# Low parts of the down weights on DVE, and weight blocks added by an accumulating load in the last three passes

## The chip, the cores and the metric

The kernel runs on one core of one Trainium2 chip. A core has TensorE (PE, matmuls; PEld is its weight load), VectorE (DVE), ScalarE (ACT), GpSimd (POOL) and SyncE (SP, which here only issues DMAs). SP's and POOL's DMAs go through two different queues, and each of those two works through its own instructions in order, as every engine does. The metric is device time of one execution in microseconds (us); lower is better.

## The reference, cut to what matters

The reference is one layer of a diffusion backbone: a token mixer, then a gated channel mixer (ConvGLU) whose result is normalised, scaled and added to the residual. The change lies in the last product, of the gated activations with the down weights. With 1024 tokens, a model width of 1024 and `D_FF` = 2816, and all arithmetic in fp32:

```python
g = silu(dwconv2d(h @ w_up[:, :D_FF])) * (h @ w_up[:, D_FF:])
y = g @ w_down                  # (1024, 2816) @ (2816, 1024)
out = x1 + gate * rmsnorm(y)
```

(The names are shortened here; the order of the operations is the reference's.)

## The kernel before

**The down projection.** It is the kernel's last stage. The product is tiled 2 by 2 over the two halves of the tokens and the two halves of the output columns, and 2 by 2 over the 2816 inner rows as well (22 blocks of 128, in two halves of `NJ` = 11). Instead of 8 products of halves it takes 7, by Strassen's scheme: `PASSES` lists for each of the 7 passes which parts of G (the gated activations) and which parts of the down weights are summed or subtracted. A pass has 11 steps, one for each block of 128 inner rows, so the stage has 77 steps, numbered n = 11 x pass + j. Two weight blocks are combined in passes 1 and 2 (a difference) and 4, 5 and 6 (a sum); two blocks of G in passes 0, 3, 4, 5 and 6.

**A step.** `prep(n)` makes the operands and `mm(n, t)` uses them. fp32 accuracy is reached by splitting each operand into a high part, rounded to the matmul's fp32r format, and a low part, the remainder, and by three matmuls for each product (`mm3`, lines 191 to 193: high x high, high x low, low x high). For each of 4 token tiles t that is 12 matmuls a step, 128 x 128 by 128 x 512. `prep(n)` issues in this order: one or two loads of a 128 x 512 weight block (256 KB) into the two halves of a buffer `raw` (line 1589, on SP's queue); where two were loaded, DVE's sum or difference into the first half (line 1591); ACT's copy of it to `wh`, the high part (line 1598); POOL's subtraction `wl` = raw - wh, the low part (line 1599, which appears in the trace as line 165, where the helper `sub_l` stands); then for G the sum on DVE (line 1603), ACT's copy (line 1606) and DVE's low part (line 165 again, with `pg` as its output).

**Buffers.** `raw` is one of the two buffers of tag `raw` (called `wr` in the trace) in every fourth step, and otherwise a page of a pool of 36 pages (`pg`), which also holds the blocks of G, their high and low parts, and the results of passes. `wh` and `wl` have four buffers each. The last six steps of pass 6 take pages for `wh` and `wl` too and are run tile by tile (all six steps for t = 0, then for t = 1, and so on), so that output tiles become ready one after the other.

**Order.** `prep` is called five steps ahead of the matmuls, the first four of them among the last steps of the up projection; a scheduler of the framework then fixes one order for each engine and the semaphores between them. Around the start of the stage DVE still computes the last 3 x 3 convolution (line 1471, nine steps in a row over the buffer `cv`), after which ACT's silu (line 1475) gives the last gated block. From pass 2 on POOL has 24 operations on results of passes (line 1448: four each of M4 - M5, C01 - C10, F + M4 and M1 + M4, and eight products with a gate). The work on results is held in a list `late`, of which a step pops one.

**Names in the rows.** `pg`, `wr` and `s`, `m`, `pad` are buffers, `ps` is a PSUM bank, `wh` and `wl` are the weights' parts, `gd` is the gated activations kept in DRAM.

Of the kernel before, what the change touches and what calls it, by code (L numbers as in the profile page):

```python
# [13 lines left out]
ALU = mybir.AluOpType  # L14
# [4 lines left out]
P = 128  # L19
# [81 lines left out]
class Kern:  # L101
# [1323 lines left out]
    def ffn(self):  # L1425
        nc, tc, A = self.nc, self.tc, self.A
        V = nc.vector
        wu = A["w_up"][0].rearrange("(k p) n -> p k n", p=P)
        with tc.tile_pool(name="ffn", bufs=1, reuse_waits="tile") as fp:
# [134 lines left out]
            def gpart(f, i):  # L1564

                if f not in here:
                    here[f] = [f >= NF - 5] * 2
                    if not here[f][0]:
                        g[f] = self.pg()
                c = slice(512 * i, 512 * i + 512)  # L1570
                if not here[f][i]:
                    nc.sync.dma_start(g[f][:, c], gd[f][:, c])
                    here[f][i] = True
                return g[f][:, c]

            def prep(n):

                ps, j = divmod(n, NJ)
                ga, wa = PASSES[ps]
                if ps == 4 and j == 0:  # L1580
                    self.gp2 = self.pg()
                    nc.sync.dma_start(self.gp2, self.gp[1])
                if n % 4:
                    raw = self.pg().rearrange("p (a n) -> p a n", a=2)
                else:
                    raw = self.wp.tile([P, 2, 512], F32, tag="raw", bufs=2, name=self.nm("wr"))
                for x, (k, c, _) in enumerate(wa):
                    f = j + NJ * k
                    nc.sync.dma_start(raw[:, x], A["w_down"][0, f * P:(f + 1) * P, 512 * c:512 * c + 512])
                if len(wa) > 1:  # L1590
                    V.tensor_tensor(raw[:, 0], raw[:, 0], raw[:, 1], op=ALU.add if wa[1][2] > 0 else ALU.subtract)
                if ps == 6 and j >= NJ - 6:
                    hl = self.page2()
                    wh, wl = hl[:, 0], hl[:, 1]
                else:
                    wh = self.wp.tile([P, 512], F32R, tag="wh", bufs=4, name=self.nm("wh"))
                    wl = self.wp.tile([P, 512], F32R, tag="wl", bufs=4, name=self.nm("wl"))
                nc.scalar.copy(wh, raw[:, 0])
                self.sub_l(nc.gpsimd, wl, raw[:, 0], wh)
                src = [gpart(j + NJ * k, i) for i, k, _ in ga]  # L1600
                if len(ga) > 1:
                    tmp = big("s") if ps == 0 else tmps[n % 4]
                    V.tensor_tensor(tmp, src[0], src[1], op=ALU.add if ga[1][2] > 0 else ALU.subtract)
                    src = [tmp]
                gs = self.page2()
                nc.scalar.copy(gs[:, 0], src[0])  # L1606
                self.sub_l(V, gs[:, 1], src[0], gs[:, 0])
                return gs, wh, wl
# [74 lines left out]
            for n, (f, p) in enumerate(seq):  # L1683
# [6 lines left out]
                x = st.setdefault(f, {})  # L1690
# [3 lines left out]
                ps = x[bank]  # L1694
                h, l = W.pop((f, p))
                for d in range(4):
                    c = slice(d * P, d * P + P)
# [24 lines left out]
                if n >= len(seq) - 4:  # L1722
                    i = len(ops)
                    ops[i] = prep(i)
            work(len(back))
            for i in range(5):
                if i not in ops:
                    ops[i] = prep(i)
# [45 lines left out]
            for ps in range(7):  # L1774
                bk = banks[BSET[ps]]
                for j in range(NJ):
                    n = ps * NJ + j
                    a = 5
                    if ps == 6 and j >= 5:
                        a += j - 5 + 1  # L1780
                    for i in range(n + 5, min(n + a, NS - 1) + 1):
                        if i not in ops:
                            ops[i] = prep(i)
                    if n < NS - 6:
                        for t in range(4):
                            mm(n, t)
                    if late and j > 0 and (ps < 6 or len(late) > 4 or j % 5 == 5 - 1):
                        late.pop(0)()
                    if ps in (5, 6) and j >= NJ - 5 and len(ahead) < 4 * (ps - 4):
                        load_x1(len(ahead))  # L1790
# [69 lines left out]
```

## Time and profile before

| | |
|---|---|
| time, median of 3 runs | 1411.86 us (1411.44 to 1413.65) |
| the profiled execution's own time | 1411.65 us |
| its span in the trace | 1409.9 us |
| mean granted clock of TensorE, whole span | 0.978 |
| the stage in question | about 1142 us to the end |

The page gives busy times over the whole span, as sums for each engine and for groups of instructions by line. The trace behind it gives the same by stretches of time, every instruction in order with the idle time before it and what ended that idle time, and for a DMA the time from issue to landing. A granted clock of 1.00 is TensorE's higher level of 2.4 GHz; a mean below it is a mix with the lower level of 1.2 GHz.

### The profile page before, as it was taken

How to read it: one execution, taken by the hardware profiler on the slowest of the kernel's cores; microseconds unless marked ns; L12 is line 12 of the kernel's file. 1: busy time of each engine (PE TensorE's matmuls, PEld its weight loads, DVE VectorE, ACT ScalarE, POOL GpSimd, SP SyncE). 2: the span in 40 equal slices, each digit the busy share in tenths (PEclk: the TensorE clock that was granted, in tenths of full speed). 3: DMA queues.
4: the chain of work that ended last, by engine and by line, in shares of the span. 5: the costliest groups of instructions: out<-in, count | busy, mean ns of one | idle time of the engine just before them, and what ended most of it. 6: DMA issues, size and time to landing. Idle time of an engine off the chain costs nothing.

```text
span 1409.9 us, 19321 instructions
## 1 busy us (share of the span) xinstructions
PE 1296.7 (92%) x6678; PEld 1028.1 (73%) x6678; DVE 1044.1 (74%) x1715; ACT 614.2 (44%) x1292; POOL 675.5 (48%) x593
## 2 busy tenths in 40 slices
PE   5999999989899999989988999999999989998685
PEld 2677876566566889877866777888888877886564
DVE  3675556836855847865688888888887899799977
ACT  5343456433543234345354344444444445454432
POOL 0440123232351354345365666666666647656773
PEclk9999999999999999999999999999999999999988
DMA  9522237676386778542403133222332285443454
GB/s 326 175 97 82 69 90 219 206 202 210 137 235 226 256 237 268 182 143 86 156 21 87 63 90 90 76 90 75 90 90 75 78 268 192 162 142 122 141 209 179
DMA packets 181427, 209.47 MB, mean 149 GB/s; under 512 B 31383, under 2 KB 119505, under 8 KB 181329
## 3 DMA queue, kind: packets, MB, share of 16 engines
q1 hardware_dynamic: 180465, 205.09, 45.2%
q0 software_dynamic: 864, 3.15, 0.7%
q8 instruction: 53, 0.87, 0.2%
q14 instruction: 45, 0.37, 0.1%
HBM read 161.01 MB, written 47.19 MB: 148 GB/s over the span
## 4 chain that ended last, share of the span: by engine, by line
PE 43%; DVE 17%; DMA 5%; issue 5%; POOL 5%; ACT 3%; SPq 0%; DVEq 0%; ACTq 0%; POOLq 0%
PE ps L191 11%; PE ps L192 11%; PE ps L193 11%; PE ps L1081 3%; POOL wl L165 2%; DVE cv L1471 2%; DVE pg L165 2%; PE ps L1025 1%; DVE T L982 1%; DVE s L1448 1%; POOL pg L165 1%; DVE pg L984 1%; PE ps L305 1%; DVE pg L1756 1%; POOL pg L1006 1%
## 5 line engine op out<-in xcount | busy, mean ns | idle before, releaser
L191 PE MATMUL ps<-pg,wh 128*128 128x512 f32 (+1 forms) x896 | 352.8, 394 | 13.2 <-ACT m L1703 10.0
L193 PE MATMUL ps<-pg,wl 128*128 128x512 f32 (+1 forms) x896 | 348.2, 389 | 0.6 <-POOL wl L165 0.6
L192 PE MATMUL ps<-pg,wh 128*128 128x512 f32 (+1 forms) x896 | 347.6, 388 | 0.0
L1471 DVE SCALAR_TENSOR_TENSOR cv<-pad,dw,cv 128x1024 f32<-128x1024 f32 x176 | 226.4, 1286 | 16.5 <-ACT cv L1469 13.1
L191 PEld LDWEIGHTS ps<-pg,wh 128*128 128x128 f32 x896 | 170.0, 190 | 62.9 <-issue 15.0
L165 POOL TENSOR_TENSOR wl<-wr,wh 128x512 fp32r<-128x512 f32 x86 | 126.2, 1472 | 179.8 <-ACT wh L183 123.7
L193 PEld LDWEIGHTS ps<-pg,wl 128*128 128x128 f32 x896 | 170.7, 190 | 37.1 <-issue 3.5
L192 PEld LDWEIGHTS ps<-pg,wh 128*128 128x128 f32 x896 | 170.7, 190 | 31.2 <-issue 0.4
L165 POOL TENSOR_TENSOR wl<-pg,wh 128x512 fp32r<-128x512 f32 x83 | 124.1, 1499 | 98.7 <-ACT wh L1641 54.1
L165 POOL TENSOR_TENSOR wl<-s,wh 128x512 fp32r<-128x512 f32 x80 | 107.4, 1344 | 54.0 <-ACT wh L1641 53.5
L192 PE MATMUL ps<-wl,pg 128*128 128x512 f32 x250 | 101.7, 407 | 22.0 <-POOL wl L165 21.9
L191 PE MATMUL ps<-wh,pg 128*128 128x512 f32 x250 | 101.0, 405 | 6.2 <-ACT pg L1606 3.5
L1641 ACT CAST wh<-s 128x512 fp32r<-128x512 f32 x80 | 49.6, 621 | 121.5 <-PE ps L192 109.5
L193 PE MATMUL ps<-wh,pg 128*128 128x512 f32 x250 | 99.6, 400 | 0.0
L193 PE MATMUL ps<-pg,pg 128*128 128x512 f32 (+1 forms) x248 | 96.7, 392 | 2.9 <-POOL pg L165 2.1
L191 PE MATMUL ps<-pg,pg 128*128 128x512 f32 (+1 forms) x248 | 97.5, 393 | 0.8 <-DVE pg L476 0.8
L192 PE MATMUL ps<-pg,pg 128*128 128x512 f32 (+1 forms) x248 | 96.4, 389 | 1.4 <-POOL pg L165 1.4
L192 PEld LDWEIGHTS ps<-wl,pg 128*128 128x128 f32 x250 | 48.5, 194 | 35.7 <-POOL wl L165 26.1
L191 PEld LDWEIGHTS ps<-wh,pg 128*128 128x128 f32 x250 | 48.6, 195 | 17.7 <-ACT pg L1606 4.0
L1081 PE MATMUL ps<-pg,pg 128*128 128x128 f32 x464 | 58.4, 277 | 2.7 <-DVE pg L1143 1.8
L1081 PEld LDWEIGHTS ps<-pg,pg 128*128 128x128 f32 x464 | 54.8, 192 | 4.6 <-DVE pg L1143 2.2
L193 PEld LDWEIGHTS ps<-pg,pg 128*128 128x128 f32 x248 | 47.0, 190 | 15.2 <-POOL pg L165 3.6
(363 smaller groups left out, 2540.5 us busy)
## 6 DMA issues: line engine op xcount, KB each, us to landing
pg<-in_w_down_dram SPq DMA_DIRECT2D x97, 256.0 KB, 4.5
wr<-in_w_ada_dram SPq DMA_DIRECT2D x32, 512.0 KB, 4.4
wr<-in_w_up_dram SPq DMA_DIRECT2D x24, 512.0 KB, 3.8
wr<-in_w_in_dram SPq DMA_DIRECT2D x20, 512.0 KB, 4.7
pg<-in_w_up_dram SPq DMA_DIRECT2D x20, 512.0 KB, 5.9
wr<-in_w_down_dram SPq DMA_DIRECT2D x35, 256.0 KB, 2.7
gd<-pg SPq DMA_DIRECT2D x17, 512.0 KB, 2.6
pg<-gd SPq DMA_DIRECT2D x34, 256.0 KB, 4.2
```

Of the source, the lines that this page charges most:

```text
L165: eng.tensor_tensor(l, full, h.bitcast(F32), op=ALU.subtract)
L191: nc.tensor.matmul(out, ah, bh, start=start, stop=False, **kw)
L192: nc.tensor.matmul(out, ah, bl, start=False, stop=False, **kw)
L193: nc.tensor.matmul(out, al, bh, start=False, stop=stop, **kw)
L305: nc.tensor.matmul(ps[32 * j:32 * j + 32, :], self.csil[:, k, :], t[:, a, :], start=(k < 4), stop=(k >= 4), skip_group_check=True, tile_po ...
L982: V.tensor_tensor(tmp, L[:nl, j + 1:, j:j + 1].broadcast_to([nl, r, c]), X[:nl, j:j + 1, 0:c].broadcast_to([nl, r, c]), op=ALU.mult)
L984: V.tensor_tensor(X[:nl, j + 1:, 0:c], X[:nl, j + 1:, 0:c], tmp, op=ALU.subtract)
L1006: nc.gpsimd.tensor_tensor(dst[:, d].rearrange("p h (b c) -> p h b c", b=4), src.unsqueeze(2).broadcast_to([P, H, 4, 32]), mask, op=ALU.mult)
L1025: nc.tensor.matmul(ps[po, h * n:(h + 1) * n], Q[k0:k0 + kn, d, h, po], R[k0:k0 + kn, d, h, c0:c0 + n], start=True, stop=True, skip_group_c ...
L1081: nc.tensor.matmul(ps[:, hs(h)], lhs(h), rhs(h), start=True, stop=True, skip_group_check=True)
L1471: V.scalar_tensor_tensor(c3, src, w, c3, op0=ALU.mult, op1=ALU.add)
L1641: nc.scalar.copy(h, src)
```

## The change

Two edits in `prep`. First, the low part `wl` of all 77 steps is subtracted by DVE in place of POOL. Second, in passes 4, 5 and 6, where two weight blocks are summed, SP loads only the first block; the second is loaded on POOL's queue by a DMA that adds what it reads to what stands in `raw[:, 0]`, and DVE's sum is left out. The second half of `raw` is then unused in those steps, but the buffer keeps its size. Passes 1 and 2, which need a difference, stay as they are. Lines from 1589 on move down by up to six: SP's load is line 1595, the adding load 1593, DVE's difference 1597, ACT's copy 1604, G's sum 1609.

```diff
--- before.py
+++ after.py
@@ -1584,10 +1584,16 @@
                     raw = self.pg().rearrange("p (a n) -> p a n", a=2)
                 else:
                     raw = self.wp.tile([P, 2, 512], F32, tag="raw", bufs=2, name=self.nm("wr"))
+
+                adds = len(wa) > 1 and ps > 3 and wa[1][2] > 0
                 for x, (k, c, _) in enumerate(wa):
                     f = j + NJ * k
-                    nc.sync.dma_start(raw[:, x], A["w_down"][0, f * P:(f + 1) * P, 512 * c:512 * c + 512])
-                if len(wa) > 1:
+                    src = A["w_down"][0, f * P:(f + 1) * P, 512 * c:512 * c + 512]
+                    if adds and x:
+                        nc.gpsimd.dma_start(raw[:, 0], src, accum_op=ALU.add)
+                    else:
+                        nc.sync.dma_start(raw[:, x], src)
+                if len(wa) > 1 and not adds:
                     V.tensor_tensor(raw[:, 0], raw[:, 0], raw[:, 1], op=ALU.add if wa[1][2] > 0 else ALU.subtract)
                 if ps == 6 and j >= NJ - 6:
                     hl = self.page2()
@@ -1596,7 +1602,7 @@
                     wh = self.wp.tile([P, 512], F32R, tag="wh", bufs=4, name=self.nm("wh"))
                     wl = self.wp.tile([P, 512], F32R, tag="wl", bufs=4, name=self.nm("wl"))
                 nc.scalar.copy(wh, raw[:, 0])
-                self.sub_l(nc.gpsimd, wl, raw[:, 0], wh)
+                self.sub_l(V, wl, raw[:, 0], wh)
                 src = [gpart(j + NJ * k, i) for i, k, _ in ga]
                 if len(ga) > 1:
                     tmp = big("s") if ps == 0 else tmps[n % 4]
```

The first place is POOL's program for the first half of pass 5. Before, its rows are the low parts of steps 1 to 7 of pass 5 and, among them, the four sums M1 + M4 of line 1448 (`wl_...` is the output, `wr_...` or `pg_...` the raw buffer).

```order
L165 TENSOR_TENSOR wl_11308<-wr_11303,wh_11307 128x512
L165 TENSOR_TENSOR wl_11334<-pg_11329,wh_11333 128x512
L1448 TENSOR_TENSOR pg_11403<-pg_11403,pg_10586 128x512 x2
L1448 TENSOR_TENSOR pg_11404<-pg_11404,pg_10587 128x512
L165 TENSOR_TENSOR wl_11360<-pg_11355,wh_11359 128x512
L1448 TENSOR_TENSOR pg_11404<-pg_11404,pg_10587 128x512
L165 TENSOR_TENSOR wl_11384<-pg_11379,wh_11383 128x512
L165 TENSOR_TENSOR wl_11414<-wr_11409,wh_11413 128x512
L165 TENSOR_TENSOR wl_11438<-pg_11433,wh_11437 128x512
L165 TENSOR_TENSOR wl_11463<-pg_11458,wh_11462 128x512
```

After, the same four sums stand among the adding loads; the buffer names tell the steps: `pg_11266`, `pg_11316`, `wr_11393`, `pg_11341` and `pg_11364` are steps 0, 2, 5, 3 and 4 of pass 5, `wr_11488` is step 9, `pg_11416`, `pg_11440` and `pg_11464` are steps 6, 7 and 8.

```order
L1593 DMA pg_11266<-in_w_down_dram 128x512
L1593 DMA pg_11316<-in_w_down_dram 128x512
L1593 DMA wr_11393<-in_w_down_dram 128x512
L1593 DMA pg_11341<-in_w_down_dram 128x512
L1593 DMA pg_11364<-in_w_down_dram 128x512
L1593 DMA wr_11488<-in_w_down_dram 128x512
L1448 TENSOR_TENSOR pg_11387<-pg_11387,pg_10586 128x512 x2
L1448 TENSOR_TENSOR pg_11388<-pg_11388,pg_10587 128x512 x2
L1593 DMA pg_11416<-in_w_down_dram 128x512
L1593 DMA pg_11440<-in_w_down_dram 128x512
L1593 DMA pg_11464<-in_w_down_dram 128x512
L1593 DMA pg_11512<-in_w_down_dram 128x512
```

What moved: the subtractions are gone from POOL, loads stand in their place, the load for step 9 is now ahead of the four sums, and the load for step 6 is behind all four.

The second place is the end of pass 6 on POOL, after the change. `wr_11694`, `pg_11717`, `pg_11740`, `pg_11762` and `wr_11799` are the buffers of steps 6 to 10; the rows of line 1448 with `pg_10995` are products of the output stage.

```order
L1593 DMA pg_11672<-in_w_down_dram 128x512
L1593 DMA wr_11694<-in_w_down_dram 128x512
L1593 DMA pg_11717<-in_w_down_dram 128x512
L1593 DMA wr_11799<-in_w_down_dram 128x512
L1448 TENSOR_TENSOR pg_11387<-pg_11387,pg_10995 128x512 x2
L1593 DMA pg_11740<-in_w_down_dram 128x512
L1448 TENSOR_TENSOR pg_11388<-pg_11388,pg_10995 128x512
L1593 DMA pg_11762<-in_w_down_dram 128x512
```

What moved: the load for step 10, whose buffer is the one that step 6 leaves, stands ahead of the loads for steps 8 and 9, and the first two products lie between.

The third place is DVE's program at the start of the stage. Before, the last convolution's operations (`cv<-pad_6494`) alternate with low parts of G and sums of G.

```order
L165 TENSOR_TENSOR pg_10040<-s_10038,pg_10040 128x512
L1471 SCALAR_TENSOR_TENSOR cv<-pad_6494,dw,cv 128x1024
L1603 TENSOR_TENSOR s_10074<-pg_9934,pg_9936 128x512
L1471 SCALAR_TENSOR_TENSOR cv<-pad_6494,dw,cv 128x1024
L1603 TENSOR_TENSOR s_10097<-pg_9969,pg_9438 128x512
L1471 SCALAR_TENSOR_TENSOR cv<-pad_6494,dw,cv 128x1024
L1603 TENSOR_TENSOR s_10120<-pg_9971,pg_9590 128x512
L1471 SCALAR_TENSOR_TENSOR cv<-pad_6494,dw,cv 128x1024
L1591 TENSOR_TENSOR wr_10230<-wr_10230 128x512
L1471 SCALAR_TENSOR_TENSOR cv<-pad_6494,dw,cv 128x1024
L1603 TENSOR_TENSOR pad_6493<-pg_9905,pg_9907 128x512
L1603 TENSOR_TENSOR pad_6494<-pg_9852,pg_9876 128x512
```

After, the first low parts of the weights (`wl_...`) stand there.

```order
L165 TENSOR_TENSOR pg_10015<-s_10013,pg_10015 128x512
L165 TENSOR_TENSOR wl_9978<-pg_9975,wh_9977 128x512
L1471 SCALAR_TENSOR_TENSOR cv<-pad_6494,dw,cv 128x1024
L165 TENSOR_TENSOR wl_10010<-pg_10007,wh_10009 128x512
L1471 SCALAR_TENSOR_TENSOR cv<-pad_6494,dw,cv 128x1024
L165 TENSOR_TENSOR wl_10035<-pg_10032,wh_10034 128x512
L1471 SCALAR_TENSOR_TENSOR cv<-pad_6494,dw,cv 128x1024
L165 TENSOR_TENSOR pg_10040<-s_10038,pg_10040 128x512
L1471 SCALAR_TENSOR_TENSOR cv<-pad_6494,dw,cv 128x1024
L165 TENSOR_TENSOR wl_10053<-wr_10050,wh_10052 128x512
L1471 SCALAR_TENSOR_TENSOR cv<-pad_6494,dw,cv 128x1024
L1609 TENSOR_TENSOR s_10074<-pg_9934,pg_9936 128x512
```

What moved: four low parts of the weights, of steps 1 to 4 of pass 0 (`wl_9978`, `wl_10010`, `wl_10035`, `wl_10053`), are between the convolution's operations now, and the difference `wr_10230` has moved behind it.

## Rows read from the trace of the kernel before

**Rows 1.** The page's first part: busy us of each engine, share of the span, instructions

```profile
PE 1296.7 (92%) x6678; PEld 1028.1 (73%) x6678; DVE 1044.1 (74%) x1715; ACT 614.2 (44%) x1292; POOL 675.5 (48%) x593
```

**Rows 2.** Busy by stretch: us, PE, PEld, DVE, ACT, POOL, PEclk, DMA share, GB/s

```profile
1150.00:1170.00 20.00, 14.74 (x57) 11.45 (x56) 18.80 (x24) 8.78 (x16) 8.81 (x5) 0.91 0.69 237
1170.00:1280.00 110.00, 110.00 (x487) 91.06 (x487) 97.34 (x86) 58.07 (x112) 72.79 (x49) 1.00 0.50 164
1280.00:1380.00 100.00, 77.03 (x303) 59.72 (x302) 88.38 (x105) 34.77 (x65) 68.88 (x40) 0.90 0.43 149
```

**Rows 3.** Timeline of ACT: start, us, what, in brackets idle before and releaser

```profile
1204.71 0.62 ACT L1598 CAST wh<-pg 128x512 fp32r<-128x512 f32 x1 [1.58 <-PE cv L193]
...
1207.43 0.62 ACT L1598 CAST wh<-pg 128x512 fp32r<-128x512 f32 x1 [1.58 <-PE cv L193]
```

**Rows 4.** PE's waits, 1100 to 1410: total us, times, longest

```profile
PE ps L192 <- POOL wl L165: 21.9, 8, 9.1
```

**Rows 5.** Timeline of PE, five starts after idling

```profile
1159.95 0.80 PE L191 MATMUL ps<-wh,pg 128*128 128x512 f32 x1 [3.53 <-ACT pg L1606]
...
1166.73 0.50 PE L192 MATMUL ps<-wl,pg 128*128 128x512 f32 x1 [1.73 <-POOL wl L165]
...
1331.50 0.50 PE L191 MATMUL ps<-wh,pg 128*128 128x512 f32 x1 [2.65 <-ACT wh L1598]
1341.08 0.80 PE L192 MATMUL ps<-wl,pg 128*128 128x512 f32 x1 [9.08 <-POOL wl L165]
...
1370.70 0.50 PE L192 MATMUL ps<-wl,pg 128*128 128x512 f32 x1 [3.34 <-POOL wl L165]
```

**Rows 6.** Timeline of DVE, beside POOL (first) and alone

```profile
1274.60 1.81 DVE L165 TENSOR_TENSOR pg<-pad,pg 128x512 fp32r<-128x512 f32 x1
...
1332.60 0.69 DVE L1591 TENSOR_TENSOR pg<-pg 128x512 f32<-128x512 f32 x1
...
1402.11 0.68 DVE L1448 TENSOR_TENSOR pg<-ps,pg 128x512 f32<-128x512 f32 x1
```

**Rows 7.** Timeline of POOL, the last row beside a busy DVE

```profile
1246.28 1.29 POOL L165 TENSOR_TENSOR wl<-pg,wh 128x512 fp32r<-128x512 f32 x1 [1.09 <-ACT wh L1598]
...
1275.82 1.74 POOL L165 TENSOR_TENSOR wl<-pg,wh 128x512 fp32r<-128x512 f32 x1
...
1331.59 9.44 POOL L165 TENSOR_TENSOR wl<-wr,wh 128x512 fp32r<-128x512 f32 x1 [5.60 <-DVE pg L1591]
```

**Rows 8.** POOL's groups, 1142 to 1384: busy us, mean ns; idle before, releasers

```profile
L165 POOL TENSOR_TENSOR wl<-pg,wh 128x512 fp32r<-128x512 f32 x53 | 84.6, 1603 | 44.5 <-ACT wh L1598 43.4 <-issue 1.1
L165 POOL TENSOR_TENSOR wl<-wr,wh 128x512 fp32r<-128x512 f32 x17 | 35.3, 2077 | 21.1 <-ACT wh L1598 14.1 <-DVE pg L1591 5.6 <-issue 1.3
```

**Rows 9.** POOL's plain loads (line 530): ns min/median/max of an issue, and landing

```profile
L530 POOL DMA_DIRECT2D pg<-in_ftab_dram x6: 527/542/722, 71.6 to 120.3; - x6
...
DMA to landing us min/median/max: 3.7/4.4/6.5
```

**Rows 10.** Line 1589, SP's loads of weight blocks

```profile
DMA to landing us min/median/max: 2.5/3.7/7.9
```

**Rows 11.** Timeline of ACT, the silu ahead of PE's first wait

```profile
1158.37 1.02 ACT L1475 ACTIVATE pg<-cv 128x1024 f32<-128x1024 f32 x1 [9.45 <-DVE cv L1471]
```

**Rows 12.** Timeline of DVE at the start of the stage

```profile
1143.60 1.72 DVE L165 TENSOR_TENSOR pg<-s,pg 128x512 fp32r<-128x512 f32 x1
...
1156.44 0.69 DVE L1591 TENSOR_TENSOR wr<-wr 128x512 f32<-128x512 f32 x1 [0.95 <-DMA wr<-in_w_down_dram]
```

**Rows 13.** Chain of waits, 950 to 1410: start, us, what ended last

```profile
1156.40 5.81 DMA pg<-in_w_down_dram
...
1163.05 3.64 POOL wl L165
```

**Rows 14.** Timeline of PE, its last matmul

```profile
1396.28 0.39 PE L193 MATMUL ps<-pg,pg 128*128 128x512 f32 x1
```

**Rows 15.** Waits of SP's queue, 1100 to 1410: total us, times, longest

```profile
SPq L1589 <- POOL wl L165: 131.2, 34, 17.5
```

## The prediction

> **What bounds the kernel now.** I read the page's busy times first: PE works 1296.7 us of a span of 1409.9, DVE 74% and POOL 48% [rows 1]. An average does not say where an edit of the down projection is felt, so next the busy times by stretch [rows 2]. From 1170 to 1280 PE starts 487 matmuls in 110 us, one per 0.226 us, and never rests: there it is the bound. A step is 12 matmuls, so 2.71 us; ACT's weight copies, each released by PE, come 2.72 us apart [rows 3]. At that pace 1150 to 1170 would hold 88.5 matmuls and holds 57, and 1280 to 1380 would hold 443 and holds 303: 31.5 and 140 are missing, which are **7.1 us and 31.6 us**. This 38.7 us is all that the change can give back ahead of the tail.
>
> What PE waits for: POOL's low parts, for 21.9 us in eight waits [rows 4]. One by one there are two waits before 1170 (3.53, 1.73) and eight from 1280 to 1380, 22.9 us together, of which three rows stand in [rows 5] beside those two. The rest of the 31.6, 8.7 us, is slow matmuls: behind the idle stretches the granted clock is at its lower level for a while, mean 0.90 there [rows 2], and matmuls take 0.50 to 0.80 us [rows 5] instead of 0.39.
>
> Why POOL is late: an operation of DVE with two operands in SBUF takes 0.68 us, or 1.8 where POOL computes beside it [rows 6]; POOL's takes 1.29 us, or 1.74 where DVE works, and at 1331.59 one took 9.44 us [rows 7], all through which DVE ran 0.69 us operations back to back [rows 6]. They take turns or one starves. In 1280 to 1380 DVE is busy 88.4 us [rows 2] with some 100 operations that alone need 0.60 to 0.68 each.
>
> **The change part by part.** *Low parts.* POOL loses 77 subtractions, 129 us by its rows from 1142 on, of which the two largest groups stand in [rows 8]. DVE gains 77. Per step DVE has 2 operations now and 3 afterwards in passes 0 to 3, and 3 before and after in passes 4 to 6, where it also loses 33 additions. Three operations back to back are 3 x 0.68 = 2.0 us of a 2.71 us step, so DVE keeps pace, now that POOL has only 24 sums and products and the issues below. A low part waits for ACT's copy, and that for PE to release the buffer of four steps before, so it has three steps, 8 us, for 0.62 + 0.68: hidden. What queues behind it on DVE are high and low parts of G four to five steps ahead.
>
> *Added by the load.* 33 transfers move from SP to POOL, which now waits for SP's first load to land, then issues. Such a load is not in this trace. POOL's own plain loads cost it 0.53 to 0.72 us each (take 0.54, the median: 33 x 0.54 = 18 us on an engine that lost 129) and land 3.7 to 6.5 us after issue [rows 9]; SP's loads of the same blocks land after 2.5 to 7.9 [rows 10]. Lower end for the landing 2.5; upper end two of the longest on POOL's queue in a row, 13.0, as the target is read too. I take 4.4, the median of the same queue.
> The Trainium skill, page "DMA: Bandwidth & Descriptors", section "Anatomy of one DMA", prices a GpSimd load at 2.0 us plus bytes over 436 GB/s, which would be 2.6 us here; the six rows above lie over it, and the sum by it would be 1 to 2 us better.
>
> Does the longer chain hide? In the built program the first load of pass 4 step 1 waits for the last matmul of pass 3 step 4, that is 7 steps or 19.0 us ahead of its use, and nearly all others have the same distance or more. The chain is 3.7 (landing, median) + 0.54 + 4.4 + 0.62 + 0.68 = 9.9 us; with the longest landings, 7.9 + 0.72 + 6.5 + 1.3 = 16.4. **Hidden either way.** Two places are tighter, because POOL's queue is in order. (a) In pass 5 four sums (M1 + M4, 1.3 to 1.74 us each) stand before the addition for step 6: issued 6 to 8 us after the pass begins, usable at 12 to 14, needed at 6 x 2.71 = 16.3. (b) In pass 6 the load for step 10 waits for step 6's low part, POOL waits for that load, and behind it stand two products and then steps 8 and 9. Walked through from the release in pass 5, step 10 is ready about 1 us after PE wants it. For (b) and what I overlooked I leave 3 us of the 31.6: **28.6 us gained**.
>
> *Start of the stage.* PE's first wait ends with ACT's silu, which had waited 9.45 us for DVE's convolution [rows 11]. On DVE that convolution gets two more operations net (1.2 us) and loses an addition's wait of 0.95 and one turn with POOL (1.72 instead of 0.68) [rows 12]: about 1 us earlier. The second wait, 1.73, is a load issued at 1156.40 that landed after 5.81 us, and then POOL's subtraction of 3.64 us [rows 13]. The load is behind the same release on SP's queue and stays, but DVE needs 0.68: the wait goes. **Gain 1.0 + 1.7 = 2.7** of 7.1; between 0, if low parts in the convolution stop DVE, and 4.
>
> *Tail.* PE's last matmul starts at 1396.28 [rows 14], while DVE reaches the sum for that tile at 1402.11 [rows 6]: DVE is the bound. From 1376 it gains six low parts (3.6 us) there or just before, loses four additions (2.4) and three turns with POOL (2.4). **Gain 1.0**, between -1 and 2.
>
> **Sum.** 2.7 + 28.6 + 1.0 = 32.3. The profiled run took 1411.65 us, 0.2 below the median of the three runs and 1.75 above its span. 1411.65 - 32.3 = 1379.35, say **1379.5 us**.
>
> **Rivals.**
> *The added load lands late (0.14).* Landing 9 to 13 us. At 13 the common chain is 18.5 us of 19.0 and loses 1 or 2 us to scatter; (a) is late by some 5 us and (b), which has two such landings in a row, by some 15. Total 20 to 22: 1390 to 1402. For it: the target must be read as well. Against it: transfers keep the queues less than half busy there [rows 2].
> *POOL's issues starve as its subtractions did (0.04).* If one of every pair of issues had to wait for DVE as at 1331.59, 9.44 us, POOL, which issues 33 times in some 95 us, would be late by some 15 us in all: about 1395. For it: [rows 7]. Against it: that starvation needed 9 us of DVE without a pause, and DVE would now pause about a third of each step; and an issue isn't an operation on SBUF data, as far as the rows tell.
> The Trainium skill, page "SBUF — State Buffer", section "SBUF: two separate sides", warns of this: while DVE runs in a two-port mode, GpSimd cannot write its descriptors, and a transfer of 620 ns took 3100. But it names DVE operations with two inputs in SBUF as a bar only to GpSimd operations that read SBUF. The second sentence agrees with [rows 6, 7]; the first would make this rival, no row here shows it, and DVE's large operations in the last passes are of the second kind.
> *Slower (0.06): the added loads become the bound.* From a landing of about 15 us (over twice the longest of POOL's) the chain passes 19.0 in each round of seven steps, 4.7 rounds in 33 steps. At 17 us a round loses 17 - 13.5 = 3.5, in all 16; (a) loses 10 and (b) 24: 50 us lost against 32 won, or less as they overlap: about 1420.
> *Nothing moves (0.03).* The waits are for buffers and not for POOL: SP's loads wait 131 us for POOL's low parts to free a buffer [rows 15], and if pages alone were short, PE would wait for a copy in place of a low part: 1409 to 1414. Against it: what frees those buffers is the very operation that gets faster.
> *The forecast (0.73).* Its own range is 1372 (all 38.7 and 1 of the tail) to 1389.
>
> **How the numbers follow.** A measurement tells 0.2%, or 2.8 us, from no change. The forecast, the late load and the starved issue are faster: 0.73 + 0.14 + 0.04 = 0.91. Same 0.03, slower 0.06. The range of 8 in 10 starts at 1372 and goes into the late loads up to 1398, the bound at 13 us nearly; beyond it are 0.03 of the late loads, 0.03 and 0.06, and a little of each end.
>
> **What would show it.** Right: no wait for a low part over 1 us after 1280 and a granted clock of 1.00 until the last steps; POOL below 65 us from 1142 on; DVE operations near 0.68 us, except beside POOL's 24; one wait of 2 to 4 us left near the start. Wrong: ACT's weight copies waiting for the POOL queue's transfer while PE idles (late loads; look first at pass 5 step 6 and at the last six steps); issues of several us on POOL (starved); longer waits on DVE ahead of the silu (start).

## Result and profile after

The changed kernel takes 1394.99 us (median of 4 runs, 1393.0 to 1397.72) against 1411.65 us before (4 runs, 1407.52 to 1413.65). The ratio is 0.9889, with a 95% interval of 0.9865 to 0.9913: **1.1% faster**, 16.7 us between the medians, where 32.3 us were forecast. The time lies inside the stated range, far from the forecast and in the window of the rival "the added load lands late". Its profiled execution took 1393.59 us with a span of 1391.8.

The page's first part, busy us of each engine (as [rows 1]):

```profile
PE 1297.6 (93%) x6673; PEld 1032.4 (74%) x6678; DVE 1006.7 (72%) x1759; ACT 615.4 (44%) x1292; POOL 571.5 (41%) x549
```

POOL has lost 104 us, and DVE, in spite of 44 more instructions, 37: but for a few places, its operations no longer take turns with POOL's. Busy times by stretch, with the columns of [rows 2] (us, PE, PEld, DVE, ACT, POOL, PEclk, DMA share, GB/s):

```profile
1150.00:1170.00 20.00, 16.94 (x68) 13.52 (x67) 19.37 (x29) 10.16 (x18) 0.00 (x0) 0.91 0.47 155
1170.00:1280.00 110.00, 110.00 (x487) 91.13 (x486) 85.82 (x125) 59.66 (x113) 18.44 (x17) 1.00 0.56 166
1280.00:1360.00 80.00, 67.51 (x270) 53.69 (x269) 60.82 (x94) 31.32 (x59) 36.54 (x35) 0.89 0.81 187
1360.00:1392.00 32.00, 17.93 (x80) 14.50 (x78) 24.66 (x59) 6.60 (x19) 7.00 (x5) 0.83 0.57 198
```

Read as in the prediction: the stretch to 1280 is unchanged, PE without a rest. From 1280 to 1360 there are 270 matmuls where 354 would fit (80 us at 0.226), so about 19 us are still lost; before it was 31.6 up to 1380 [rows 2]. The DMA engines are 0.81 busy there, at 187 GB/s; the kernel before has 0.48 and 166 GB/s in the same stretch. PE's waits from 1100 on (total us, times, longest):

```profile
PE ps L191 <- ACT wh L1604: 7.1, 1, 7.1
PE ps L192 <- DVE wl L165: 5.3, 2, 4.0
PE ps L191 <- ACT pg L1612: 3.1, 1, 3.1
```

No wait for POOL is left [rows 4]. The 3.1 us are the silu at the start, which the prediction left standing. The other three are new, in the timeline of PE (start, us, what; in brackets the idle time before and what ended it) together with its last matmul:

```profile
1289.48 0.79 PE L192 MATMUL ps<-wl,pg 128*128 128x512 f32 x1 [4.02 <-DVE wl L165]
...
1315.76 0.50 PE L192 MATMUL ps<-wl,pg 128*128 128x512 f32 x1 [1.32 <-DVE wl L165]
...
1345.07 0.79 PE L191 MATMUL ps<-wh,pg 128*128 128x512 f32 x1 [7.13 <-ACT wh L1604]
...
1377.54 0.39 PE L193 MATMUL ps<-pg,pg 128*128 128x512 f32 x1
```

To set the runs side by side I use two figures of each profiled execution. **Lost time** is what the spacing of PE's matmul starts has over 0.227 us, waits and low clock together, summed from 1140 to 1180 (start) and from 1270 to the end (passes 4 to 6). **Stage** is the span less the start of the matmul that the silu releases, 1159.95 before [rows 5] and 1158.21 after; it leaves out what differs earlier, where that moment lay between 1157.7 and 1162.9 in all but one of the executions shown below, with the same program up to there.

(Each ratio is to the runs of the kernel before on the same chip; the last three columns are from one profiled execution each.)

| kernel | sums of results on | adding loads in passes | median us | ratio, 95% interval | lost at start | lost in passes 4 to 6 | stage |
|---|---|---|---|---|---|---|---|
| before | POOL | none (low parts on POOL) | 1411.65 | 1 | 7.5 | 34.2 | 249.9 |
| the change | POOL | 4 to 6 | 1394.99 | 0.9889 (0.9865 to 0.9913) | 5.5 | 19.2 | 233.6 |
| e1_low_only | POOL | none | 1389.89 | 0.9848 (0.9832 to 0.9864) | 4.0 | 15.7 | 226.8 |
| e2_add_only | POOL | 4 to 6 (low parts on POOL) | 1422.75 | 1.0084 (1.0064 to 1.0104) | 6.8 | 48.2 | 262.1 |
| e3_sums_dve | DVE | 4 to 6 | 1384.18 | 0.9816 (0.9769 to 0.9862) | 5.5 | 6.8 | 220.5 |
| e3b_sums4_dve | DVE in pass 4, else POOL | 4 to 6 | 1383.29 | 0.9794 (0.9770 to 0.9818) | 4.6 | 8.3 | 221.2 |
| e5_add_45 | POOL | 4, 5 | 1391.84 | 0.9858 (0.9839 to 0.9878) | 5.5 | 18.8 | 230.6 |
| e7_overwrite | POOL | 4 to 6, writing | 1384.03 | 0.9808 (0.9787 to 0.9828) | 5.4 | 9.3 | 224.1 |
| e8_copy_order | POOL | 4 to 6 | 1396.36 | 0.9908 (0.9871 to 0.9944) | 5.5 | 20.2 | 233.4 |
| e10_sums_low | DVE | none | 1383.97 | 0.9804 (0.9785 to 0.9823) | 5.5 | 3.9 | 223.3 |
| e11_sums_add45 | DVE | 4, 5 | **1377.77** | 0.9761 (0.9738 to 0.9785) | 4.8 | 5.9 | 217.7 |
| e13_x1_late | POOL | 4 to 6 | 1396.66 | 0.9895 (0.9877 to 0.9912) | 6.8 | 17.4 | 233.7 |
| e14_sums_not_last6 | DVE | 4, 5, half of 6 | 1383.66 | 0.9791 (0.9768 to 0.9814) | 5.5 | 6.8 | 220.6 |
| e16_sums_x1_late | DVE | 4 to 6 | 1380.49 | 0.9787 (0.9770 to 0.9805) | 5.2 | 3.3 | 218.2 |

By these the change gained 2.0 us at the start, 15.0 in passes 4 to 6, and lost 0.7 in the tail (last matmul to end: 13.6 before, 14.3 after), 16.3 of the 18.1 us between the two spans; the rest lies before the stage. Against the forecast 0.7 us are missing at the start, 13.6 in passes 4 to 6 and 1.7 in the tail. What is still lost in passes 4 to 6, 19.2 us, is lost in two places.

**First place: DVE stands beside POOL's sums.** The timelines of DVE and of POOL:

```profile
1269.90 6.02 DVE L165 TENSOR_TENSOR wl<-pg,wh 128x512 fp32r<-128x512 f32 x1
...
1283.14 1.79 DVE L1448 TENSOR_TENSOR s<-s,pg 128x512 f32<-128x512 f32 x1 [1.21 <-POOL pg L1448]
1284.86 3.37 DVE L1609 TENSOR_TENSOR pad<-pg 128x512 f32<-128x512 f32 x1
...
1288.75 0.68 DVE L165 TENSOR_TENSOR wl<-pg,wh 128x512 fp32r<-128x512 f32 x1
...
1309.85 5.85 DVE L165 TENSOR_TENSOR wl<-pg,wh 128x512 fp32r<-128x512 f32 x1 [2.62 <-ACT wh L1604]
```

```profile
1268.40 1.90 POOL L1593 DMA_DIRECT2D pg<-in_w_down_dram  x2
1269.99 2.87 POOL L1448 TENSOR_TENSOR pg<-s,m 128x512 f32<-128x512 f32 x2
1272.54 2.81 POOL L1448 TENSOR_TENSOR pg<-pg,pg 128x512 f32<-128x512 f32 x2
...
1280.89 3.50 POOL L1448 TENSOR_TENSOR pg<-s,m 128x512 f32<-128x512 f32 x2 [0.97 <-DVE pad L1609]
1284.33 0.83 POOL L1593 DMA_DIRECT2D wr<-in_w_down_dram  x1
1284.94 2.73 POOL L1448 TENSOR_TENSOR pg<-pg,pg 128x512 f32<-128x512 f32 x2
...
1309.23 0.88 POOL L1593 DMA_DIRECT2D wr<-in_w_down_dram  x1 [4.53 <-DMA wr<-in_w_down_dram]
1309.79 5.35 POOL L1448 TENSOR_TENSOR pg<-pg,pg 128x512 f32<-128x512 f32 x4
```

Pass 4 begins at about 1269. Where DVE's low part takes 6.02 us, POOL runs four sums back to back (two of C01 - C10, two of F + M4); at 1309.85, early in pass 5, the same again with M1 + M4. The low part that PE waits 4.02 us for is a later one: its weight copy was made at 1277.1 and it starts at 1288.75. Ahead of it on DVE stand a product that sat idle for 1.21 us until one of POOL's next four sums (1280.89 to 1287.67) was done and then took 1.79, and a sum of G that took 3.37 beside the last two of them. Behind the stall at 1309.85 stands the wait of 1.32. With the slow matmuls after each, 9.1 us are lost from 1280 to 1320.

**Second place: a copy in pass 6 waits for an adding load.** The timeline of ACT and, of the chain that ended last, the two transfers ahead of it:

```profile
1343.88 0.62 ACT L1604 CAST pg<-pg 128x512 fp32r<-128x512 f32 x1 [14.36 <-DMA pg<-in_w_down_dram]
1344.40 0.61 ACT L1604 CAST wh<-pg 128x512 fp32r<-128x512 f32 x1
```

```profile
1324.16 12.91 DMA pg<-in_w_down_dram
...
1338.18 5.62 DMA pg<-in_w_down_dram
```

ACT sits idle for 14.36 us before a copy whose block landed at 1343.8. That copy is step 5's of pass 6; it goes to a page, so it waits for no weight buffer, and the scheduler has put it **ahead of step 0's copy**, whose block had been complete for over ten us. PE needs step 0. And step 5's load is late because POOL, in order, waits for step 4's first load to land before it adds to it, and that load took 12.91 us. With slow matmuls behind, 10.1 us are lost from 1330 to 1350. Two stretches, with the columns of [rows 2], show why a load takes that long:

```profile
1320.00:1330.00 10.00, 10.00 (x45) 8.26 (x44) 10.00 (x17) 6.42 (x11) 1.75 (x2) 1.00 1.08 281
1330.00:1340.00 10.00, 7.94 (x35) 6.19 (x33) 2.65 (x5) 0.00 (x0) 4.07 (x5) 1.00 1.04 291
```

The DMA engines are full. Four residual loads of 512 KB (line 1739) are issued between 1316 and 1324, among the weights.

### The profile page after: what moved, and what is told of

Its sections match the earlier page's. It is cut to its first block, busy times and chain, and to the rows that moved or that the text cites. A ratio compares the mean times of both kernels' runs of the same rounds, so it can differ in the third digit from the quotient of the medians.

```text
span 1391.8 us, 19249 instructions
## 1 busy us (share of the span) xinstructions
PE 1297.6 (93%) x6673; PEld 1032.4 (74%) x6678; DVE 1006.7 (72%) x1759; ACT 615.4 (44%) x1292; POOL 571.5 (41%) x549
## 4 chain that ended last, share of the span: by engine, by line
PE 46%; DVE 16%; issue 6%; DMA 5%; POOL 3%; ACT 3%; SPq 0%; DVEq 0%; ACTq 0%; POOLq 0%
PE ps L191 12%; PE ps L193 11%; PE ps L192 11%; PE ps L1081 4%; DVE cv L1471 3%; DMA pg<-in_w_down_dram 2%; DVE s L1448 2%; PE ps L1025 1%; DVE pg L165 1%; PE ps L305 1%; DVE pg L1762 1%; POOL pg L1006 1%; PE ps L1012 1%; POOL wl L165 1%; DVE wl L165 1%
## 5 line engine op out<-in xcount | busy, mean ns | idle before, releaser
L165 POOL TENSOR_TENSOR wl<-wr,wh 128x512 fp32r<-128x512 f32 x68 | 90.0, 1330 | 161.6 <-ACT wh L183 128.3
L1448 POOL TENSOR_TENSOR pg<-pg,pg 128x512 f32<-128x512 f32 x20 | 28.2, 1503 | 85.7 <-ACT pg L1810 64.3
L165 POOL TENSOR_TENSOR wl<-pg,wh 128x512 fp32r<-128x512 f32 x30 | 39.7, 1324 | 56.9 <-ACT wh L1647 56.9
L165 DVE TENSOR_TENSOR wl<-pg,wh 128x512 fp32r<-128x512 f32 x53 | 47.6, 900 | 14.6 <-ACT wh L1604 14.5
```

Source lines behind the costliest of these rows:

```text
L165: eng.tensor_tensor(l, full, h.bitcast(F32), op=ALU.subtract)
L1448: eng.tensor_tensor(o, a, b, op=op)
```

## Experiments

### Each half of the change alone

Low parts on DVE, no adding loads:

```diff
-                adds = len(wa) > 1 and ps > 3 and wa[1][2] > 0
+                adds = False
```

> Half of the change: the low parts are on DVE, and all second blocks come by SP's queue and are added by DVE as before. Theory A (what is left of the waits in the changed kernel comes from the adding loads: the copies of pass 6 wait 7.1 us for one, and with the slow matmuls behind it 10 us are lost there): without such loads this time goes, DVE copes, 1383 to 1388. Theory B (DVE is the scarce engine in passes 4 to 6, and what is left comes from its stalls beside POOL's sums, where two low parts took 6.0 and 5.9 us): DVE now has four operations of 0.60 us in each of 33 steps, 79 us, and some 16 of its own on results and 10 us of stalls, against 89 us of matmuls, so it is late by 15 us or more: 1395 to 1405.

1389.89 us, in neither range, and its interval lies below that of the change, if only just: the moved low parts are worth more than the whole change, and **the adding loads cost 5 us on top**. Why not more? DVE and POOL still meet at the same sums, as DVE's timeline and then POOL's show:

```profile
1270.89 1.77 DVE L165 TENSOR_TENSOR pg<-pad,pg 128x512 fp32r<-128x512 f32 x1
1272.59 1.80 DVE L165 TENSOR_TENSOR wl<-pg,wh 128x512 fp32r<-128x512 f32 x1
1274.31 1.78 DVE L1597 TENSOR_TENSOR pg<-pg 128x512 f32<-128x512 f32 x1
```

```profile
1270.66 3.18 POOL L1448 TENSOR_TENSOR pg<-s,m 128x512 f32<-128x512 f32 x2 [55.81 <-PE cv L193]
1273.80 3.45 POOL L1448 TENSOR_TENSOR pg<-pg,pg 128x512 f32<-128x512 f32 x2
```

Here they take turns, 1.8 us for each of DVE's operations, and PE's waits after 1170 are

```profile
PE ps L192 <- DVE wl L165: 6.6, 2, 4.0
```

so POOL's sums hold DVE up whether it is for one long operation or for several shorter ones: 11.2 us are lost from 1280 to 1320, more than the 9.1 of the change. There is no wait for a weight copy in pass 6.

The adding loads alone:

```diff
-                self.sub_l(V, wl, raw[:, 0], wh)
+                self.sub_l(nc.gpsimd, wl, raw[:, 0], wh)
```

> The other half: second blocks are added by the loads on POOL's queue in passes 4 to 6, and POOL keeps the low parts. Theory A (the adding loads are what costs): slower than the changed kernel, and little better than before, 1400 to 1412. Theory B (DVE's operations and POOL's are in each other's way): DVE loses 33 operations, POOL gains 33 issues of 0.9 us on top of 33 low parts of 1.3 to 1.7 and 24 sums of 1.5, together some 110 to 120 us in 89 us of matmuls, so POOL is the bound: 1400 to 1415 as well, but with PE waiting for low parts and not for copies. A time under 1395 would say that the adding load alone is the gain.

1422.75 us, **slower than before**, by more than either theory said. PE's waits after 1170:

```profile
PE ps L192 <- POOL wl L165: 19.5, 7, 7.2
PE ps L191 <- ACT wh L1604: 5.3, 5, 2.7
```

POOL now has low parts, sums and issues in one queue, and low parts late as before [rows 4], with waits for copies added. So the gain of the change is the low parts' move, not the loads.

### The sums on DVE

All 16 (one line shown of four alike):

```diff
-   ... tt(nc.gpsimd, M["F"][t], M["F"][t], M["M4"][t]) ...
+   ... tt(V, M["F"][t], M["F"][t], M["M4"][t]) ...
```

> The changed kernel with POOL's 16 sums and differences of results (M4 - M5, C01 - C10, F + M4, M1 + M4) on DVE, so that POOL has only the issues and the eight products at the end. Two things change: no POOL operation stands beside the low parts, and the copy for step 5 of pass 6 now stands behind that for step 0 on ACT. Theory B (stalls beside POOL's sums): no low part takes over 1 us, the waits of 4.0 and 1.3 us and 9 us of lost matmul time go, and 1.0 us or so of DVE's own is added: 1384 to 1387, and 1376 to 1380 if the order on ACT takes the third wait along. Theory A (the loads are what costs): low parts of 0.7 us, but the same time as the changed kernel but for ACT's order, 1388 to 1395.

1384.18 us, 10.8 less than the change. What PE waits for after 1170:

```profile
PE ps L191 <- ACT wh L1604: 3.7, 1, 3.7
PE ps L192 <- DVE wl L165: 0.4, 1, 0.4
```

No stall, no wait to speak of for a low part: theory B. The wait for a copy is still there, half as long. To see that it is the sums and not the copy's order, which had changed with them, only the eight sums that POOL has in pass 4 were moved in the next run, with the copies in the changed kernel's order:

> The changed kernel with only the eight sums of pass 4's end (C01 - C10 and F + M4) on DVE; M4 - M5 and M1 + M4 stay on POOL, and the order of ACT's copies in pass 6 is that of the changed kernel. Theory B (a low part stood 6.0 us beside four such sums, and PE's wait of 4.0 us with the slow matmuls behind it, 7.2 us in all, follows from that): that stall and that wait go, the second stall (5.9 us beside M1 + M4) and the wait for a copy in pass 6 stay: 1386 to 1390. Theory F (DVE is simply full there, and the place of the sums doesn't matter): the wait moves by a step or so but stays, 1393 to 1397.

1383.29 us, 3 us better than expected:

```profile
PE ps L191 <- ACT wh L1604: 5.6, 1, 5.6
```

The waits for low parts are gone, both of them. One operation of DVE still took 5.87 us beside M1 + M4, but PE had no wait behind it. So with the sums of pass 4 the second wait went too. Theory F, a full DVE, falls.

Then no adding loads either (the edits of e1 and e3 together):

> No adding loads, and POOL out of the way: low parts, weight sums and the 16 sums of results are all on DVE, POOL has eight products at the end. If the two engines' turns are what cost (theory B), DVE's operations take 0.60 us each; 4 in each of 33 steps are 79 us, and about 36 on results 22 us, 101 us against 89 us of matmuls: with what is prepared ahead DVE comes out some 5 to 10 us late, 1384 to 1391. If DVE is not late (the steps prepared ahead take it up), 1377 to 1381.

1383.97 us. PE loses only 3.9 us in passes 4 to 6, the least but one, and yet the time is no better, for its last matmul is here:

```profile
1361.76 0.39 PE L193 MATMUL ps<-pg,pg 128*128 128x512 f32 x1
```

From there to the end of the span (1381.0) are 19.2 us, against 13.6 before: DVE's late work comes out in the output's tail. This is the use that the adding loads have: they take 33 operations off DVE, and with them in passes 4 and 5 alone (e11 below) the tail is 12.3 us and the time 6.2 us less.

### The adding loads

The same loads without the addition, so that passes 4 to 6 use the second block alone:

```diff
-                        nc.gpsimd.dma_start(raw[:, 0], src, accum_op=ALU.add)
+                        nc.gpsimd.dma_start(raw[:, 0], src)
```

> The changed kernel, but the loads on POOL's queue only write and do not add, so that passes 4 to 6 use the second weight block alone in place of the sum; the order, the waits and the bytes read are the same. Theory D (adding itself takes DMA time: the transfers kept the DMA engines 0.81 busy from 1280 to 1360 at 187 GB/s, while the kernel with DVE's adds had 0.53 at 184): the share falls to 0.55 to 0.65, the loads land after 3 to 4 us and not 5.6, the wait of 7.1 us at the copies of pass 6 shrinks to 0 to 3, and the time is 1386 to 1391; DVE's stalls beside POOL's sums stay. Theory E (the chain of two loads one after the other, in order on POOL, is what costs, whatever the second load does): 1393 to 1397, as the changed kernel.

1384.03 us, 11 us less than the change, more than theory D expected. The issue and landing of these loads, in the changed kernel and then here (line 1593, ns min/median/max of an issue):

```profile
L1593 POOL DMA_DIRECT2D pg<-in_w_down_dram x24: 863/885/2280, 1255.9 to 1356.5; - x24
...
DMA to landing us min/median/max: 3.7/5.6/12.4
```

```profile
L1593 POOL DMA_DIRECT2D pg<-in_w_down_dram x24: 536/538/579, 1259.9 to 1351.5; - x24
...
DMA to landing us min/median/max: 2.8/3.4/7.2
```

The page's line on POOL's queue, of the change and of this run (packets, MB, share of 16 engines' span):

```profile
q0 software_dynamic: 5616, 11.80, 4.5%
```

```profile
q0 software_dynamic: 3504, 11.80, 2.7%
```

Less the 0.7% of 1409.9 us that the queue had before (9.9 us), the 33 loads took 52.8 us of all 16 engines with the addition and 27.6 without: **1.6 against 0.8 us each**. By stretch:

```profile
1280.00:1360.00 80.00, 74.55 (x313) 60.20 (x312) 69.40 (x112) 34.45 (x65) 28.35 (x36) 0.96 0.60 201
```

The share falls from 0.81 to 0.60 while more bytes move, step 5's copy runs at 1338.9 and not 1343.9, and the 7.1 us wait is 1.1. DVE, POOL, ACT and SP run their operations in the changed kernel's order. Adding is what makes these loads late; the two loads in a row, which are the same here, are not enough for it.

The order of the copies: step 5 of pass 6 takes the usual buffer.

```diff
-                if ps == 6 and j >= NJ - 6:
+                if ps == 6 and j > NJ - 6:
```

> The changed kernel, but step 5 of pass 6 takes the usual buffers for its high and low part and not a page. Its copy on ACT, which stood ahead of the copy for step 0 and waited for a load that landed at 1343.8, then stands behind that for step 4; the copy for step 6 still stands ahead of that for step 1. Theory C (the 7.1 us wait is the order of ACT's copies, since the block of step 0 itself had landed at 1331.1): PE gets a step's 2.7 us of work more before it waits for step 6's copy, and the wait is 4 to 5 us: 1390 to 1393. Theory A (the loads are late for every step): no change, 1393 to 1397.

1396.36 us, no gain. Step 0's copy now ran in time, but step 6's, ahead of step 1's, waited 13.85 us for its load, and PE 6.5 us for step 1:

```profile
1357.49 0.62 ACT L1604 CAST pg<-wr 128x512 fp32r<-128x512 f32 x1 [13.85 <-DMA wr<-in_w_down_dram]
```

One place in the order decides only which load is waited for; theory C gave the mechanism and not the price.

No adding loads in pass 6:

```diff
-                adds = len(wa) > 1 and ps > 3 and wa[1][2] > 0
+                adds = len(wa) > 1 and 3 < ps < 6 and wa[1][2] > 0
```

> The changed kernel with adding loads in passes 4 and 5 only; pass 6 loads both blocks by SP and DVE adds them; the sums of results stay on POOL. Theory A/D (the third wait of the changed kernel, 7.1 us with 10 us lost in all, is late adding loads): that wait goes, the stalls of DVE beside POOL's sums and their waits (4.0 and 1.3 us, 9 us lost) stay, and 1 to 4 us come back in pass 6 from DVE's extra work: 1385 to 1390. Rival (the work on DVE in pass 6 costs as much as the late loads did): 1392 to 1397.

1391.84 us, between the two ranges. The copies' wait is gone, but the one behind M1 + M4 is 4.1 us here and was 1.3. Up to that wait DVE, POOL, ACT and SP run their operations in the changed kernel's order, so the edit did not make it grow; it differs between executions:

```profile
PE ps L192 <- DVE wl L165: 8.3, 2, 4.2
PE ps L191 <- ACT pg L1612: 1.9, 1, 1.9
```

The residual's four loads out of the way of pass 6:

```diff
-                    if ps in (5, 6) and j >= NJ - 5 and len(ahead) < 4 * (ps - 4):
+                    if ps == 6 and j >= NJ - 5 and len(ahead) < 4 * (ps - 4):
```

> The changed kernel, but the four loads of the residual (512 KB each, line 1739), which SP issues between 1316 and 1324, while the weights of pass 6 are loaded, come only when an output tile needs them; the order of ACT's copies is the changed kernel's. Theory G (the DMA engines are full there: busy share 1.04 to 1.08 from 1320 to 1340, and step 4's first load landed 12.9 us after issue): that load lands in 5 to 8 us, the wait of 7.1 us shrinks to 1 to 3 us, and the time is 1388 to 1392 unless the late residual loads delay the output. Theory E (the chain in order on POOL costs by itself): the wait stays over 5 us, 1393 to 1397.

1396.66 us. The wait for the copy shrinks to 2.7 us, as theory G said, but the time is no better. The waits for low parts are longer, and two of the three (4.35 and 2.87 us, where the change had 4.02 and 1.32) lie ahead of the edit, as in the run before:

```profile
PE ps L192 <- DVE wl L165: 8.3, 3, 4.3
PE ps L191 <- ACT wh L1604: 2.7, 1, 2.7
```

So the same was tried with the sums on DVE, where these stalls are gone:

> The version with the 16 sums on DVE and adding loads in passes 4 to 6 (1384.2), with the four residual loads of pass 5 taken when the output needs them. DVE has no stall that could take a gain back. The copy for step 5 of pass 6 stands ahead of that for step 0 on ACT here, as in the changed kernel, which by itself would make the wait longer. Theory G (full DMA engines make the loads of pass 6 late): the wait of 3.7 us for a copy in pass 6 goes to 0 to 2 us, 1377 to 1382. Theory E (the chain in order on POOL is enough): the wait stays at 3.7 or grows to 5 to 7 us, 1384 to 1389.

1380.49 us; no wait for a copy, and PE's waits after 1170 are down to

```profile
PE ps L192 <- DVE pg L165: 1.2, 1, 1.2
PE ps L192 <- DVE wl L165: 1.1, 1, 1.1
```

The stage is 2.3 us shorter than e3's, in spite of the worse order of copies. The intervals of the two overlap, so it is the vanished wait and not the time that speaks for theory G.

### Two versions put together

Sums on DVE, adding loads in passes 4 and 5:

> The 16 sums on DVE, adding loads in passes 4 and 5 only; in pass 6 the second blocks come by SP and DVE adds them. Theory A/D (late adding loads among the residual's loads make the 3.7 us wait in pass 6 that is left with the sums on DVE): no wait for a copy in pass 6, 6 us less, 1376 to 1380. Rival: DVE, with four operations a step in pass 6 and the output's work beside them, is late there: 1384 to 1390.

1377.77 us, the best of all, 17 us below the change with an interval clear of it. PE's waits after 1170:

```profile
PE ps L191 <- ACT pg L1612: 1.9, 1, 1.9
PE ps L192 <- DVE wl L165: 0.6, 1, 0.6
```

(The 1.9 us are for a part of G at the end.) With adding loads also in the first five steps of pass 6:

> The 16 sums on DVE, adding loads in passes 4 and 5 and in the first five steps of pass 6, DVE's adds in the last six. If DVE's work in pass 6 is what is left in the version with adding loads in passes 4 and 5 only (1377.8), 1374 to 1377; if the DMA engines are (share near 1 while the residual is loaded), or ACT's copies of the last six stand ahead of earlier ones and wait, 1380 to 1386.

1383.66 us: the second forecast. A wait for a copy, 1.8 us, is back, and the stage is 2.9 us longer than with passes 4 and 5 alone; the intervals of the two times just overlap. No run shows a gain from adding loads in pass 6.

## Why the prediction was wrong

**What bounds the kernel: right.** PE's waits for POOL's low parts were what could be had, and moving them gave it; without the move the kernel is slower (e2). POOL's rest came to 63.3 us after 1142 (below 65 was said).

**Start: nearly right.** 2.0 instead of 2.7: the wait of 1.73 went as forecast, the silu's shrank from 3.53 to 3.06, half a us and not a whole one (the terms in the prediction add up to 0.8).

**Low parts: "DVE keeps pace" is the step that failed first.** I made the sum with 0.68 us for each of three operations a step, and dismissed POOL's 24 sums and products as few. [rows 6, 7] had shown that such operations of the two engines exclude each other; I priced not even the single turn (1.8 us) of those rows, and left out that four sums follow each other twice in pass 4 and once more in pass 5, and that DVE has eight products of its own in pass 4, one of which even waited for a sum of POOL's. The row of 9.44 us in [rows 7] was the warning: an engine can be held for a whole run of the other's operations. I read it as a weakness of POOL, and for its mirror image on DVE named no rival. Price: 9.1 us lost; e3b and e3 show it by taking the sums away (8.3 and 6.8 us lost in passes 4 to 6, for 19.2).

The Trainium skill, page "SBUF — State Buffer", section "SBUF: two separate sides", says of the port pair that the two share that who starts first has it for the whole instruction. The trace agrees that one of them is fully held, and differs in the rest: DVE's 6.02 us began, by the records, 0.09 us before the first of four of POOL's sums and lasted through all four.

**"Hidden either way" failed in pass 6.** Both terms of the chain were low: an issue took 0.89 us for 0.54, more than the longest row that I had (0.72); a landing 5.6 for 4.4 at the median and 12.4 at most, inside the 13.0 that I had allowed. SP's load ahead of them took up to 12.91 us, where 7.9 was the longest row. The places I had named as tight, step 6 of pass 5 and step 10 of pass 6, made PE wait nowhere, though my sign for late loads, a weight copy in the last six steps that waits for POOL's queue, did show. The error was in what a late load holds up. I counted 19 us from the buffer's release to a block's own use; ACT's order puts page steps' copies ahead of others, so a load has to land before the copies *behind* its own are due. I checked POOL's order and not ACT's. And I took the DMA share of before, 0.43 [rows 2], for the share after: an adding load takes twice the DMA time of a writing one (e7), and the residual's loads come on top (e16). Price: 10.1 us lost; with loads that only write (e7) passes 4 to 6 lose 9.3 us in all.

**Tail:** +1.0 was forecast, -0.7 came, inside the bounds that were given.

**Rivals.** That the time lies in the window of "the added load lands late" is in part luck: late loads took 10.1 of the 19.2 us that are still lost, through a mechanism other than the rival's own (landings of 9 to 13 us throughout), and DVE's stalls, which no rival held, the other 9.1. "Issues starve" did not happen: the median issue took 0.89 us beside a DVE that was busy for 60.8 of 80 us, and what an issue takes beyond 0.54 is the addition's: in e7 no issue took over 0.60 us. The Trainium skill, page "SBUF — State Buffer", section "SBUF: two separate sides", names DVE operations with two inputs in SBUF as a bar only against GpSimd operations that read SBUF, and these issues agree. That the second edit by itself costs time (e1 against the change) stood only in the rivals (0.14, 0.04 and 0.06); the forecast had it as hidden.

When DVE and POOL take turns and when DVE is held, the traces show by counting. From 1142 us on, in the traces of all fourteen kernels, 25 sums, differences and products of DVE (128 x 512) took over 1.9 us beside POOL, 2.05 to 8.97, and in each case POOL's operations beside it had begun no more than 0.05 us after the end of a DMA issue on POOL. Beside operations of POOL that did not follow an issue so closely, none took over 1.81 us. The changed kernel has both within a few us: 1.79 beside the sums at 1280.89, and 3.37 beside the two at 1284.94, right behind the issue of 1284.33. In e1, where POOL issues nothing, there are only turns; in e7, whose loads only write, one finds 5.89, 3.11 and 6.02 us. So the long holds of DVE go with an issue just ahead, adding or not.

What stays open: why an issue brings this about, and why POOL was held for 9.44 us [rows 7] in a stage in which it issued nothing. Nor does a run have all of pass 6's copies in the order of the steps, which would show what the loads cost without ACT's order.

## What to carry to other kernels

Before moving work to an engine, look at which operations of the other engine exclude it, and count them in runs: four in a row, right behind a DMA issue, held DVE for all four, and what stands behind in its queue is late long after. When a wait becomes a longer chain, follow every in-order queue that the chain passes, the copy's too: the latest block in front decides, not a block's own slack. And try the parts of a change alone, here one of the two gave more than both.

## What the runs showed of the hardware

An adding load of 256 KB took 1.6 us of all 16 DMA engines where one that only writes took 0.8, and 0.89 against 0.54 us of POOL's time to issue; from 1320 to 1340 the engines were full at 281 to 291 GB/s. Subtractions and sums with both operands in SBUF held each other off for up to 9.4 us on POOL [rows 7] and 6.0 us on DVE in the changed kernel (8.97 in e2); on DVE over 1.9 us only where POOL's operations came right behind a DMA issue.
